# Two transformer blocks on one core: the expert routing's lists are moved behind each query part, and the expert buffers are laid out before it

## Chip, core and metric

One core of a Trainium2 chip runs the whole program. The metric is the device time of one execution in microseconds (us), the median of the runs. Names of engines: PE is TensorE (matmuls), PEld its weight loads, DVE is VectorE, ACT is ScalarE, POOL is GpSimd, SP is SyncE, which issues nearly all transfers.

## What is computed

Two transformer blocks in a row over 512 tokens of 1024 features, in float32. The first block mixes tokens by neighbourhood attention and a gated recurrence (HGRN2), and then applies a feed-forward part of 16384 experts with product keys (PEER). The change lies in this last part, in the reference:

```python
q = (t @ wq).reshape(128, 8, 2, 128)                      # queries: 8 heads, 2 halves
s = jnp.einsum('tpcd,pckd->tpck', q, sub_keys)            # scores against 128 sub-keys per half
s1, i1 = lax.top_k(s[:, :, 0], 16)
s2, i2 = lax.top_k(s[:, :, 1], 16)
cand = (s1[..., :, None] + s2[..., None, :])...           # 256 candidates per head
top, pos = lax.top_k(cand, 16)                            # 16 experts per head, 128 per token
g = jax.nn.softmax(top, axis=-1)
a = jax.nn.gelu(jnp.einsum('tpkd,td->tpk', u[idx], t), approximate=False)
return jnp.einsum('tpk,tpkd->td', (g * a), v[idx])
```

The modulation vectors of both blocks (products of a conditioning vector with `w_mod` and `w_ada`) are computed between other work. The second block (stick-breaking attention and latent attention) follows and isn't touched.

## The kernel before

The tokens are four blocks of 128 (`b` 0 to 3). Three of them (`ND` = 3, blocks 0 to 2) go through all experts densely: for each of 128 groups `e` of 128 experts, `s_part(e)` loads the group's `uT`, splits it into a high part (ACT, L190) and a low part (DVE, L191), and takes 24 matmuls of 384 columns, whose GELU is `S`. The first 88 groups' `S` are stored to DRAM (`sd`), the rest stay in the `NS` buffers of the pool `sbufS`. Block 3 is gathered: `gather` fetches the rows of `u` and `v` of its 128 experts per token with indirect transfers from POOL (`uv`, four buffers), and DVE takes the dot products and the weighted sums.

Every fp32 weight is loaded in tiles of 512 KB into a ring of four buffers named `wr` and split into `wh` and `wl`, rings of four as well. `wload` uses it for the queries' weights, `s_part` for the experts' `uT`, the last stage for `v`. A `wr` buffer comes free when its tile is split.

The order in the program is: three products (`EARLY` = 3); then eight query parts `j`, each with 48 matmuls of 512 columns (`pqT`), the scores of the four blocks (`keysT`, copied to `rsc` by ACT), and, for odd `j`, one modulation vector by `gemv_T`, whose eight weight tiles come through a ring of its own (`wg`, two buffers), two halves being summed in PSUM, copied to `row` by ACT and turned into columns by matmuls with `pick`; then 49 products up to `PRE` = 52; then the routing of blocks 3, 2, 1, 0. Routing takes the 16 best of each of a block's 16 lists (`top16`: five DVE operations and three loads of match values), then of the candidates, then the softmax (an Exp on ACT, L780), and transposes what it selected (`sel`, `gt_`) on PE into `selT`. Next is the one-hot stage (`pG`, 12 parts, with three products and one pair of gathered experts each), which builds the dense gate matrix and stores it to DRAM (`gd`); then some products ahead of the last stage; then the last stage (`po`): 128 groups of 18 matmuls of 512 columns with `v`.

The Tile scheduler makes each engine's queue at compile time from a model of its own. The program's order is the priority: an instruction that has its inputs and a buffer by that model is taken before all that stand behind it in the program. On the chip each queue runs in that order, and an instruction that waits holds up all behind it. `tc.issue_after(x)` puts what it encloses behind `x` on the engine of `x`.

A pool's memory is taken when it is opened and given back when it is closed; `reuse_waits="tile"` makes a new tile wait only for the old tiles under it. In the kernel before, the pool of the gather buffers is opened after the routing's pool `eR` is closed, so that they share memory.

Of the kernel before, what the change touches and what calls it, by code (L numbers as in the profile page):

```python
# [18 lines left out]
P = 128  # L19
# [3 lines left out]
D = 1024  # L23
KT = D // P
# [97 lines left out]
DRAM = bass.MemoryType.DRAM  # L122
BF16 = mybir.dt.bfloat16
NDENSE = 3
NS = 10
NSP = 88
PRE = 52
GEN = 3
GR = 1
LAST = 4  # L130
MOD_ORDER = (0, 5, 1, 6, 2, 7, 3, 4)
EARLY = 3
# [3 lines left out]
def program(tc, a, out, tap=None):  # L136
# [35 lines left out]
    DMA.dma_start(cs.rearrange("p a b -> p (a b)"), a["cs"])  # L172
    DMA.dma_start(vecs, a["vecs"])

    def mm(ps, lhs, rhs, first=True, last=True):
        PE.matmul(ps, lhs, rhs, start=first, stop=last)  # L176

    class Split:
        def __init__(self, hi, lo):
# [64 lines left out]
        for i in range(4):  # L244
            mm(ps[32 * i:32 * i + 32, :], cvec[:, 3 * (k0 + i):3 * (k0 + i) + 32], w[:, i, :], k0 == 0, k0 == 4)

    def gemv_T(pl, ps_pool, wname, part, v, slot, bias, tag="pm"):
        row = pl.tile([P, D], F32, name="row", bufs=1)
        for h2 in range(2):
            ps = ps_pool.tile([P, 512], F32, name=tag)  # L250
            for h in range(2):
                hf = 2 * h2 + h
                for k0 in (0, 4):
                    w = pl.tile([P, 4, GW], F32, name="wg", bufs=2)
                    DMA.dma_start(w.rearrange("p k n -> p (k n)"), a[wname][4 * part + hf][:, k0 * GW:(k0 + 4) * GW])
                    gemv_rows(ps[:, h * GW:(h + 1) * GW], w, k0)
            S.copy(row[:, h2 * 512:(h2 + 1) * 512], ps)
        ps = ps_pool.tile([P, 512], F32, name=tag)[:, :2 * KT].rearrange("p (k o) -> p k o", o=2)
        for kt in range(KT):
            mm(ps[:, kt, :], row[:, kt * P:(kt + 1) * P], pick[:, v:v + 2])  # L260
        V.tensor_add(modT[:, slot, :], ps[:, :, 0], bias)

    def bcast(ps_pool, dst, colT):
        for hf in range(2):
# [418 lines left out]
    def s_part(e, elo=None):  # L683
        u_ = wpool["w"].tile([P, KT, P], F32, name="wr")
        DMA.dma_start(u_.rearrange("p a b -> p (a b)"), a["uT"][e])
        hi = wpool["w"].tile([P, KT, P], F32R, name="wh")
        lo = wpool["w"].tile([P, KT, P], F32R, name="wl")
        split(u_, hi, lo, S.copy, elo)
        ps = pS.tile([P, 512], F32, name="pS3")
        for kt in range(KT):  # L690
            mm(ps[:, :nd], hi[:, kt, :], h2T.hi[:, kt, :nd], kt == 0, False)
            mm(ps[:, :nd], hi[:, kt, :], h2T.lo[:, kt, :nd], False, False)
            mm(ps[:, :nd], lo[:, kt, :], h2T.hi[:, kt, :nd], False, kt == KT - 1)
        r = sbuf.tile([P, nd], F32, name="S")
        S.activation(r, ps[:, :nd], AF.Gelu)  # L695
        return r

    for e in range(EARLY):
        DMA.dma_start(sd[e], s_part(e, V.tensor_tensor))
    eR = ExitStack()  # L700
    tp = pool(eR, "tp2", 1, PSUM)
    pm = pool(eR, "pm2", 4, PSUM)
# [10 lines left out]
    V.memset(zer, 0.0)  # L713

    def top16(src, w, val, pos):
        t = r2.tile([P, P], F32, name="mr", bufs=2)[:, :w]
        V.max(val[:, 0:8], src)
        V.max_index(pos[:, 0:8], val[:, 0:8], src)
        V.match_replace(t, val[:, 0:8], src, -3e38)
        V.max(val[:, 8:16], t)  # L720
        V.max_index(pos[:, 8:16], val[:, 8:16], t)

    REG = ((0, 1, 16, 0), (1, 3, 8, 16), (4, 4, 4, 40), (8, 8, 1, 56))

    def routing(b, sc):
        sv = r2.tile([P, 16, 16], F32, name="sv", bufs=2)
        si = r2.tile([P, 16, 16], U32, name="si", bufs=2)
        for j in range(16):
            top16(sc[:, j, :], P, sv[:, j, :], si[:, j, :])
        sif = r2.tile([P, 8, 2, 16], BF16, name="sif")  # L730
        V.tensor_copy(sif.rearrange("p a b c -> p (a b) c"), si)
        cand = r2.tile([P, 8, 64], F32, name="cand")
# [34 lines left out]
        V.tensor_copy(abb.rearrange("p s h k -> p s (h k)"), ab)  # L767
        sel = []
        for s_ in range(2):
            eq = r2.tile([P, 8, 16, 16], BF16, name="eq", bufs=2)  # L770
# [4 lines left out]
            t = r2.tile([P, 8, 16], F32, name=f"sel{s_}")  # L775
# [8 lines left out]
        gt_ = gate[b] if b in gate else r2.tile([P, P], F32, name="gt_")  # L784
        V.tensor_tensor(gt_.rearrange("p (h k) -> p h k", k=16), tm, ts_[:, :, None].to_broadcast([P, 8, 16]), op=OP.mult)
        if b in idx:
            V.scalar_tensor_tensor(sel[0], sel[0], 128.0, sel[1], op0=OP.mult, op1=OP.add)
            V.tensor_copy(idx[b], sel[0])
        else:
            ps = tp.tile([P, 512], F32, name="tp").rearrange("p (k c) -> p k c", k=4)  # L790
            for j, t in enumerate((sel[0], sel[1], gt_)):
                PE.transpose(ps[:, j, :], t, ident)
            S.copy(selT[b], ps[:, :3, :])

    scs = [rb.tile([P, 16, P], F32, name=f"rsc{i}") for i in range(NB)]
    for j in range(8):
        qT = r2.tile([P, 2, T], F32, name="pqT", bufs=2)
        w = wload("wq", j)
        for m in range(2):
            ps = pm.tile([P, 512], F32, name="pm")  # L800
            proj_T(ps, w, m * P, P, h2T, 0, T)
            S.copy(qT[:, m, :], ps)
        for i in range(NB):
            ps = pm.tile([P, 512], F32, name="pm")
            for m in range(2):
                mm(ps[:, m * P:(m + 1) * P], qT[:, m, i * P:(i + 1) * P], keysT[:, 2 * j + m, :])
            S.copy(scs[i][:, 2 * j:2 * j + 2, :].rearrange("p a b -> p (a b)"), ps[:, :GW])
        if j == 1:
            gemv_T(rb, tp, "w_mod", 5, 0, 5, bmT[:, 40:48], "tp")
        elif j % 2:  # L810
            part = j // 2 - 1
            gemv_T(rb, tp, "w_ada", part, 2, 6 + part, baT[:, part * 8:part * 8 + 8], "tp")
    V.scalar_tensor_tensor(modT[:, 7, :], modT[:, 7, :], 1.0, ng2T, op0=OP.add, op1=OP.mult)
    V.tensor_mul(modT[:, 7, :], modT[:, 7, :], nfT)
    for e in range(EARLY, PRE):
        DMA.dma_start(sd[e], s_part(e))
    for b in reversed(range(NB)):
        routing(b, scs[b])
    eR.close()

    ug = pool(eM, "uvg", 1)
    nfB = ug.tile([P, D], F32, name="nfB")
    DMA.dma_start(nfB, a["rows"][0:1, :].to_broadcast([P, D]))
    S.activation(nfB, nfB, AF.Square)
    gt2 = ug.tile([P, D], F32, name="gt2")
    eU = ExitStack()
    up = pool(eU, "uv", 4)
    acc = {b: ug.tile([P, D], F32, name=f"pacc{b}") for b in range(ND, NB)}
    dts = {b: ug.tile([P, P], F32, name=f"dts{b}") for b in range(ND, NB)}
    scr = ug.tile([P, D], F32, name="pscr")  # L830
    for b in acc:
        V.memset(acc[b], 0.0)
    GRP = 2

    def gather(b, j0):
        tl = []
        for j in range(j0, j0 + GRP):
            uv = up.tile([P, 2 * D], F32, name="uv")
            G.indirect_dma_start(out=uv, out_offset=None, in_=a["uv"], in_offset=bass.IndirectOffsetOnAxis(ap=idx[b][:, j:j + 1], axis=0))  # L839
            V.scalar_tensor_tensor(scr, uv[:, :D], 1.0, h2g[b], op0=OP.mult, op1=OP.mult, accum_out=dts[b][:, j:j + 1])  # L840
            tl.append(uv)
        ds_ = dts[b][:, j0:j0 + GRP]
        S.activation(ds_, ds_, AF.Gelu)
        V.tensor_mul(ds_, ds_, gate[b][:, j0:j0 + GRP])
        for j in range(j0, j0 + GRP):
            V.scalar_tensor_tensor(acc[b], tl[j - j0][:, D:], dts[b][:, j:j + 1], acc[b], op0=OP.mult, op1=OP.add)  # L846

    todo = [(b, j0) for b in range(ND, NB) for j0 in range(0, P, GRP)]
    prog = [0]

    def run_gather(upto):
        for k in range(prog[0], min(upto, len(todo))):
            gather(*todo[k])
        prog[0] = max(prog[0], upto)

    with ExitStack() as es:
        gg = pool(es, "ggen", 2)
# [2 lines left out]
        for b in range(ND):  # L860
            i1_, i2_, g_ = (selT[b][:, k, :] for k in range(3))
            for tg in range(4):
# [40 lines left out]
    with ExitStack() as es:  # L903
# [16 lines left out]
        for n, e in enumerate(order):  # L920
# [346 lines left out]
```

## Time and profile before

| | |
|---|---|
| median of 3 runs | 2346.18 us (2343.89 to 2346.5) |
| profiled execution | 2337.86 us, span 2336.1 us |
| mean granted clock of TensorE | 0.992 |
| PE busy | 97% of the span |
| DVE, ACT, POOL busy | 68%, 42%, 11% |

The profile is of one execution. Busy shares are means over stages with different limits. The matmuls are pipelined and their ends are modelled, so PE's idle time in a stretch, and the count of its matmuls there, say more than its busy share.

### The profile page before, as it was taken

Reading aid. Unit: us, or ns where it says so; the run is one execution under the profiler, and the core shown is the slowest. Engines: PE = TensorE matmul, PEld = TensorE weight load, DVE = VectorE, ACT = ScalarE, POOL = GpSimd, SP = SyncE. Lnnn points to the kernel's source line nnn. Section 1 sums busy time; section 2 is a strip of 40 time slices with the busy share of each in tenths; the row PEclk is TensorE's granted clock in tenths of the full one; section 3 lists DMA queues with packets and bytes.
Section 4 is the critical chain, followed back from the end, with each engine's and each line's share of the span. In section 5 each row is a group of like instructions: output and inputs, shape, how many; then the busy total and the mean of one; then the engine's idle time right before and its main releaser. Section 6 shows DMA issues by size and latency. Waiting matters only on the chain. (4 is left out here: it accounts for less than half of the span.)

```text
span 2336.1 us, 34601 instructions
## 1 busy us (share of the span) xinstructions
PE 2259.9 (97%) x13097; PEld 1942.3 (83%) x13097; DVE 1598.4 (68%) x3193; ACT 980.3 (42%) x1828; POOL 249.1 (11%) x159
## 2 busy tenths in 40 slices
PE   7999999998999999999999999999999999989998
PEld 4899986597779999999988888888888786666888
DVE  3674723354359977999689888888898627767344
ACT  4432333333234335877534333333333434446421
POOL 0000000000000000322222222222130000000000
PEclk9999999999999999999999999999999999999999
DMA  7111135625555574999999999999997231120221
GB/s 265 55 57 55 52 118 178 212 101 178 165 196 158 163 258 153 328 320 319 333 360 396 406 347 349 354 362 363 360 380 263 88 103 42 50 86 28 98 92 55
DMA packets 170871, 481.74 MB, mean 206 GB/s; under 512 B 14864, under 2 KB 87952, under 8 KB 153168
## 3 DMA queue, kind: packets, MB, share of 16 engines
q1 hardware_dynamic: 152272, 345.31, 42.7%
q0 software_dynamic: 18432, 134.23, 14.7%
q8 instruction: 103, 1.69, 0.3%
q14 instruction: 64, 0.52, 0.1%
HBM read 431.76 MB, written 46.66 MB: 205 GB/s over the span
## 5 line engine op out<-in xcount | busy, mean ns | idle before, releaser
L191 DVE TENSOR_TENSOR wl<-wr,wh 128x1024 fp32r<-128x1024 f32 (+1 forms) x378 | 456.7, 1211 | 362.3 <-ACT wh L190 359.8
L190 ACT CAST wh<-wr 128x1024 fp32r<-128x1024 f32 (+1 forms) x378 | 394.0, 1043 | 440.4 <-PE pm L176 196.1
L176 PE MATMUL pS<-h2h,wh 128*128 128x384 f32 x1024 | 348.2, 340 | 7.3 <-ACT S L695 7.2
L176 PE MATMUL pS<-h2h,wl 128*128 128x384 f32 x1024 | 346.1, 338 | 0.0
L176 PE MATMUL pS<-h2l,wh 128*128 128x384 f32 x1024 | 345.5, 337 | 0.0
L839 POOL DMA_INDIRECT uv<-in_uv_dram,idx x128 | 225.8, 1764 | 1006.9 <-DVE pacc L846 688.8
L176 PE MATMUL po<-wl,Wh 128*128 128x512 f32 x768 | 299.6, 390 | 1.8 <-DVE wl L191 1.8
L176 PE MATMUL po<-wh,Wl 128*128 128x512 f32 x768 | 299.5, 390 | 0.0
L176 PE MATMUL po<-wh,Wh 128*128 128x512 f32 x768 | 298.9, 389 | 0.0
L176 PEld LDWEIGHTS pS<-h2h,wh 128*128 128x128 f32 x1024 | 193.4, 189 | 11.7 <-ACT S L695 8.7
L176 PEld LDWEIGHTS pS<-h2l,wh 128*128 128x128 f32 x1024 | 193.3, 189 | 2.0 <-issue 0.8
L176 PEld LDWEIGHTS pS<-h2h,wl 128*128 128x128 f32 x1024 | 193.2, 189 | 0.0
L190 ACT CAST Wh<-W 128x384 fp32r<-128x384 f32 x128 | 65.7, 513 | 267.8 <-PE po L176 162.1
L176 PE MATMUL pm<-h2h,wh 128*128 128x512 f32 x432 | 173.5, 402 | 0.2 <-ACT cr L1106 0.2
L176 PE MATMUL pm<-h2h,wl 128*128 128x512 f32 x432 | 171.8, 398 | 0.0
L176 PE MATMUL pm<-h2l,wh 128*128 128x512 f32 x432 | 171.8, 398 | 0.0
L176 PEld LDWEIGHTS po<-wl,Wh 128*128 128x128 f32 x768 | 144.1, 188 | 31.9 <-DVE wl L191 2.6
L176 PEld LDWEIGHTS po<-wh,Wl 128*128 128x128 f32 x768 | 144.1, 188 | 30.3 <-DVE Wl L191 0.3
L176 PEld LDWEIGHTS po<-wh,Wh 128*128 128x128 f32 x768 | 144.2, 188 | 29.2
L846 DVE SCALAR_TENSOR_TENSOR pacc<-uv,dts,pacc 128x1024 f32<-128x1024 f32 x128 | 163.9, 1281 | 1.9
L840 DVE SCALAR_TENSOR_TENSOR pscr<-uv,h 128x1024 f32<-128x1024 f32 x128 | 156.1, 1219 | 1.9 <-DMA uv<-in_uv_dram,idx 0.9
L191 DVE TENSOR_TENSOR Wl<-W,Wh 128x384 fp32r<-128x384 f32 x128 | 70.8, 553 | 47.9 <-ACT Wh L190 47.8
(410 smaller groups left out, 4100.6 us busy)
## 6 DMA issues: line engine op xcount, KB each, us to landing
wr<-in_uT_dram SPq DMA_DIRECT2D x128, 512.0 KB, 6.0
wr<-in_uv_dram SPq DMA_DIRECT2D x128, 512.0 KB, 7.7
gd<-stg SPq DMA_DIRECT2D x12, 2048.0 KB, 12.6
Gt<-gd SPq DMA_DIRECT2D x32, 768.0 KB, 8.4
sd<-S SPq DMA_DIRECT2D x88, 192.0 KB, 3.9
Sr<-sd SPq DMA_DIRECT2D x88, 192.0 KB, 6.8
wr<-in_w_in_dram SPq DMA_DIRECT2D x32, 512.0 KB, 3.6
wg<-in_w_mod_dram SPq DMA_DIRECT2D x32, 512.0 KB, 4.3
```

The lines of the kernel that those rows point to most:

```text
L176: PE.matmul(ps, lhs, rhs, start=first, stop=last)
L190: (ehi or S.copy)(hi, src)
L191: (elo or V.tensor_tensor)(lo, src, hi.bitcast(F32), op=OP.subtract)
L839: G.indirect_dma_start(out=uv, out_offset=None, in_=a["uv"], in_offset=bass.IndirectOffsetOnAxis(ap=idx[b][:, j:j + 1], axis=0))
L840: V.scalar_tensor_tensor(scr, uv[:, :D], 1.0, h2g[b], op0=OP.mult, op1=OP.mult, accum_out=dts[b][:, j:j + 1])
L846: V.scalar_tensor_tensor(acc[b], tl[j - j0][:, D:], dts[b][:, j:j + 1], acc[b], op0=OP.mult, op1=OP.add)
```

## The change

The eight query parts with their scores stay in front, and the 16-best lists of all four blocks are now taken behind each part, not in the routing; the routing keeps what follows the lists and runs in the order 3, 0, 1, 2. The scores need eight small buffers (`rsc`, 1 KB per partition each) where they had four of 8 KB. The pools of the gather (`uv`, the sums and two broadcast rows) are opened before the routing's, and four pairs of experts are gathered ahead of the one-hot stage (`G0`). The transposes of blocks 0, 1 and 2 are put behind the products 34, 44 and 51 on PE. To make room, `sbufS` has 6 buffers for 10, the modulation's weight tiles go through `wr` (in the routing stage; in the attention stage they keep `wg`), `row` is half as wide and each half is turned into columns before the next half begins, the dot product is written over the gathered row, and some small tiles have one buffer for two, or two for one (`sel`, `gt_`).

```diff
-NS = 10
+NS = 6
+G0 = 4
+G1 = G0 + GR * 4 * NDENSE
+BORDER = (3, 0, 1, 2)
+NLIST = 8
+HOLD = (34, 44, 51)
...
+        last_mm[0] = PE.matmul(ps, lhs, rhs, start=first, stop=last)
...
-    def gemv_T(pl, ps_pool, wname, part, v, slot, bias, tag="pm"):
-        row = pl.tile([P, D], F32, name="row", bufs=1)
+    def gemv_T(pl, ps_pool, wname, part, v, slot, bias, tag="pm", share=False):
...
-                    w = pl.tile([P, 4, GW], F32, name="wg", bufs=2)
+                    w = wpool["w"].tile([P, 4, GW], F32, name="wr") if share else pl.tile([P, 4, GW], F32, name="wg", bufs=2)
...
-            S.copy(row[:, h2 * 512:(h2 + 1) * 512], ps)
-        ps = ps_pool.tile([P, 512], F32, name=tag)[:, :2 * KT].rearrange("p (k o) -> p k o", o=2)
-        for kt in range(KT):
-            mm(ps[:, kt, :], row[:, kt * P:(kt + 1) * P], pick[:, v:v + 2])
-        V.tensor_add(modT[:, slot, :], ps[:, :, 0], bias)
+            row = pl.tile([P, 512], F32, name="row", bufs=1)
+            S.copy(row, ps)
+            ps = ps_pool.tile([P, 512], F32, name=tag)[:, :KT].rearrange("p (k o) -> p k o", o=2)
+            for k in range(4):
+                mm(ps[:, k, :], row[:, k * P:(k + 1) * P], pick[:, v:v + 2])
+            V.tensor_add(modT[:, slot, 4 * h2:4 * h2 + 4], ps[:, :, 0], bias[:, 4 * h2:4 * h2 + 4])
...
+    ug = pool(eM, "uvg", 1)
...
+    up = pool(eU, "uv", 4)
...
-            V.scalar_tensor_tensor(scr, uv[:, :D], 1.0, h2g[b], op0=OP.mult, op1=OP.mult, accum_out=dts[b][:, j:j + 1])
+            V.scalar_tensor_tensor(uv[:, :D], uv[:, :D], 1.0, h2g[b], op0=OP.mult, op1=OP.mult, accum_out=dts[b][:, j:j + 1])
...
     eR = ExitStack()
...
-    def routing(b, sc):
-        sv = r2.tile([P, 16, 16], F32, name="sv", bufs=2)
-        si = r2.tile([P, 16, 16], U32, name="si", bufs=2)
-        for j in range(16):
-            top16(sc[:, j, :], P, sv[:, j, :], si[:, j, :])
+    def routing(b):
+        sv, si = svs[b], sis[b]
...
-            for j, t in enumerate((sel[0], sel[1], gt_)):
-                PE.transpose(ps[:, j, :], t, ident)
+            with tc.issue_after(after[HOLD[b]].ins):
+                for j, t in enumerate((sel[0], sel[1], gt_)):
+                    PE.transpose(ps[:, j, :], t, ident)
...
-        for i in range(NB):
+        lists = []
+        for i in BORDER:
...
-            S.copy(scs[i][:, 2 * j:2 * j + 2, :].rearrange("p a b -> p (a b)"), ps[:, :GW])
+            sc = r2.tile([P, 2, P], F32, name="rsc", bufs=NLIST)
+            S.copy(sc.rearrange("p a b -> p (a b)"), ps[:, :GW])
+            lists.append((i, sc))
...
-            gemv_T(rb, tp, "w_ada", part, 2, 6 + part, baT[:, part * 8:part * 8 + 8], "tp")
+            gemv_T(rb, tp, "w_ada", part, 2, 6 + part, baT[:, part * 8:part * 8 + 8], "tp", True)
+        for i, sc in lists:
+            for m in range(2):
+                top16(sc[:, m, :], P, svs[i][:, 2 * j + m, :], sis[i][:, 2 * j + m, :])
...
     for e in range(EARLY, PRE):
         DMA.dma_start(sd[e], s_part(e))
-    for b in reversed(range(NB)):
-        routing(b, scs[b])
+        after[e] = last_mm[0]
+    for b in BORDER:
+        routing(b)
+    run_gather(G0)
     eR.close()
...
-                    run_gather(GR * (b * 4 + tg + 1))
+                    run_gather(G0 + GR * (b * 4 + tg + 1))
...
-                run_gather(GR * ND * 4 - (GR * ND * 4 - len(todo)) * (n + 1) // (P - 10))
+                run_gather(G1 + (len(todo) - G1) * (n + 1) // (P - 10))
```

## Rows read from the trace of the kernel before

**Rows 1.** The page, part 1: busy us, share, instructions.

```profile
PE 2259.9 (97%) x13097; PEld 1942.3 (83%) x13097; DVE 1598.4 (68%) x3193; ACT 980.3 (42%) x1828; POOL 249.1 (11%) x159
```

**Rows 2.** Stretches: length, busy PE PEld DVE ACT POOL (instructions), clock, DMA share, GB/s.

```profile
547.50:697.50 150.00, 145.64 (x896) 109.85 (x894) 61.57 (x288) 46.00 (x80) 0.00 (x0) 1.00 0.54 177
697.50:840.00 142.50, 139.12 (x793) 138.48 (x794) 141.92 (x643) 54.39 (x73) 5.48 (x4) 0.99 0.54 163
840.00:905.00 65.00, 65.00 (x378) 64.65 (x377) 33.35 (x69) 22.43 (x32) 0.00 (x0) 1.00 0.64 230
905.00:935.00 30.00, 27.58 (x180) 26.30 (x179) 28.00 (x36) 25.18 (x56) 1.84 (x2) 1.00 0.50 166
935.00:1145.00 210.00, 209.79 (x1434) 206.48 (x1433) 195.71 (x202) 168.31 (x415) 63.39 (x21) 1.00 0.95 324
...
1260.00:1800.00 540.00, 540.00 (x2536) 465.89 (x2535) 475.61 (x656) 202.38 (x314) 129.10 (x85) 1.00 0.94 359
```

**Rows 3.** Groups of PE instructions, 560 to 700 us: the modulation's matmuls.

```profile
L176 PE MATMUL tp<-wg,cvec 128*32 128x256 f32 x248 | 21.0, 389 | 4.4 <-DMA wg<-in_w_ada_dram 2.9 <-DMA wg<-in_w_mod_dram 1.4
```

**Rows 4.** ACT in order of time at the third Exp of the routing.

```profile
784.27 1.28 ACT L780 ACT_TABLE_LOAD   x1
791.48 0.31 ACT L780 ACTIVATE tm<-tm 128x128 f32<-128x128 f32 x1 [5.92 <-DVE tm L779]
```

**Rows 5.** Stretches around idle time of PE, columns as in rows 2.

```profile
466.00:468.00 2.00, 0.25 (x3) 0.13 (x2) 0.83 (x2) 2.00 (x5) 0.00 (x0) 1.00 0.89 297
468.00:472.00 4.00, 4.00 (x22) 4.00 (x23) 4.00 (x7) 3.45 (x7) 0.00 (x0) 0.57 0.63 246
790.00:795.00 5.00, 1.70 (x10) 1.38 (x9) 5.00 (x31) 3.50 (x5) 0.00 (x0) 1.00 0.48 157
795.00:800.00 5.00, 5.00 (x22) 5.00 (x21) 5.00 (x21) 0.85 (x2) 0.00 (x0) 0.66 0.45 109
```

**Rows 6.** PE in order of time: waits at the one-hot stage's start and end.

```profile
923.85 2.53 PE L176 MATMUL pG<-Rh,Lq 128*128 128x128 f32 x16 [0.98 <-ACT Lq L879]
927.45 0.44 PE L176 MATMUL pS<-h2h,wh 128*128 128x384 f32 x1 [1.07 <-ACT S L695]
...
1169.36 0.45 PE L176 MATMUL pS<-h2h,wh 128*128 128x384 f32 x1 [2.81 <-ACT S L695]
```

**Rows 7.** Groups of DVE instructions, 550 to 950 us: count, busy us, mean ns, idle before.

```profile
L191 DVE TENSOR_TENSOR wl<-wr,wh 128x1024 fp32r<-128x1024 f32 x70 | 85.1, 1218 | 101.6 <-ACT wh L190 101.4
...
L718 DVE FIND_INDEX8 si<-sv,rsc 128x8 uint32<-128x128 f32 x64 | 18.1, 283 | 0.0
...
L717 DVE MAX8 sv<-rsc 128x8 f32<-128x128 f32 x64 | 16.1, 281 | 8.9 <-ACT rsc L807 8.9
...
L846 DVE SCALAR_TENSOR_TENSOR pacc<-uv,dts,pacc 128x1024 f32<-128x1024 f32 x4 | 5.1, 1276 | 0.0
L840 DVE SCALAR_TENSOR_TENSOR pscr<-uv,h 128x1024 f32<-128x1024 f32 x4 | 4.9, 1219 | 0.0
```

**Rows 8.** ACT in order of time around the modulation vector of part 1.

```profile
572.37 1.05 ACT L190 CAST wh<-wr 128x1024 fp32r<-128x1024 f32 x1 [1.67 <-PE pm L176]
...
578.92 0.59 ACT L257 COPY row<-tp 128x512 f32<-128x512 f32 x1 [2.98 <-PE tp L176]
```

**Rows 9.** PE in order of time, the same place.

```profile
573.16 1.06 PE L176 MATMUL tp<-wg,cvec 128*32 128x256 f32 x14
574.16 1.38 PE L176 MATMUL pm<-keysT,pqT 128*128 128x128 f32 x10
578.22 0.64 PE L176 MATMUL tp<-wg,cvec 128*32 128x256 f32 x8 [0.83 <-DMA wg<-in_w_mod_dram]
...
590.42 1.84 PE L176 MATMUL tp<-pick,row 128*128 128x2 f32 x16
```

**Rows 10.** SP's queue in order of time, last stage, groups 11 and 12.

```profile
1213.52 0.33 SPq L931 DMA_DIRECT2D wr<-in_uv_dram  x1
1217.54 0.33 SPq L685 DMA_DIRECT2D wr<-in_uT_dram  x1
```

**Rows 11.** DMA issues, 547.5 to 697.5 us: count, KB, median us to landing.

```profile
wr<-in_uT_dram SPq DMA_DIRECT2D x10, 512.0 KB, 4.7
wr<-in_wq_dram SPq DMA_DIRECT2D x9, 512.0 KB, 4.7
```

More of the change, by code (lines that the diff above doesn't have):

```diff
@@ L173, in program @@
     DMA.dma_start(vecs, a["vecs"])
+    last_mm = [None]
     def mm(ps, lhs, rhs, first=True, last=True):
-        PE.matmul(ps, lhs, rhs, start=first, stop=last)
+        last_mm[0] = PE.matmul(ps, lhs, rhs, start=first, stop=last)
     class Split:
@@ L699, in program, with gather, run_gather @@
         DMA.dma_start(sd[e], s_part(e, V.tensor_tensor))
+    ug = pool(eM, "uvg", 1)
+    nfB = ug.tile([P, D], F32, name="nfB")
+    DMA.dma_start(nfB, a["rows"][0:1, :].to_broadcast([P, D]))
+    S.activation(nfB, nfB, AF.Square)
+    gt2 = ug.tile([P, D], F32, name="gt2")
+    acc = {b: ug.tile([P, D], F32, name=f"pacc{b}") for b in range(ND, NB)}
+    eU = ExitStack()
+    up = pool(eU, "uv", 4)
+    ux = pool(eU, "uvx", 1)
+    dts = {b: ux.tile([P, P], F32, name=f"dts{b}") for b in range(ND, NB)}
+    for b in acc:
+        V.memset(acc[b], 0.0)
+    GRP = 2
+    def gather(b, j0):
+        tl = []
+        for j in range(j0, j0 + GRP):
+            uv = up.tile([P, 2 * D], F32, name="uv")
+            G.indirect_dma_start(out=uv, out_offset=None, in_=a["uv"], in_offset=bass.IndirectOffsetOnAxis(ap=idx[b][:, j:j + 1], axis=0))
+            V.scalar_tensor_tensor(uv[:, :D], uv[:, :D], 1.0, h2g[b], op0=OP.mult, op1=OP.mult, accum_out=dts[b][:, j:j + 1])
+            tl.append(uv)
+        ds_ = dts[b][:, j0:j0 + GRP]
+        S.activation(ds_, ds_, AF.Gelu)
+        V.tensor_mul(ds_, ds_, gate[b][:, j0:j0 + GRP])
+        for j in range(j0, j0 + GRP):
+            V.scalar_tensor_tensor(acc[b], tl[j - j0][:, D:], dts[b][:, j:j + 1], acc[b], op0=OP.mult, op1=OP.add)
+    todo = [(b, j0) for b in range(ND, NB) for j0 in range(0, P, GRP)]
+    prog = [0]
+    def run_gather(upto):
+        for k in range(prog[0], min(upto, len(todo))):
+            gather(*todo[k])
+        prog[0] = max(prog[0], upto)
     eR = ExitStack()
@@ L715, in top16 @@
     def top16(src, w, val, pos):
-        t = r2.tile([P, P], F32, name="mr", bufs=2)[:, :w]
+        t = r2.tile([P, P], F32, name="mr", bufs=1)[:, :w]
         V.max(val[:, 0:8], src)
@@ L723, in program @@
     REG = ((0, 1, 16, 0), (1, 3, 8, 16), (4, 4, 4, 40), (8, 8, 1, 56))
-    def routing(b, sc):
-        sv = r2.tile([P, 16, 16], F32, name="sv", bufs=2)
-        si = r2.tile([P, 16, 16], U32, name="si", bufs=2)
-        for j in range(16):
-            top16(sc[:, j, :], P, sv[:, j, :], si[:, j, :])
+    svs = [rb.tile([P, 16, 16], F32, name=f"sv{b}") for b in range(NB)]
+    sis = [rb.tile([P, 16, 16], U32, name=f"si{b}") for b in range(NB)]
+    def routing(b):
+        sv, si = svs[b], sis[b]
         sif = r2.tile([P, 8, 2, 16], BF16, name="sif")
@@ L769, in routing @@
         for s_ in range(2):
-            eq = r2.tile([P, 8, 16, 16], BF16, name="eq", bufs=2)
+            eq = r2.tile([P, 8, 16, 16], BF16, name="eq", bufs=1)
             V.tensor_tensor(eq, abb[:, s_][:, :, None, :].to_broadcast([P, 8, 16, 16]), iob[:, None].to_broadcast([P, 8, 16, 16]), op=OP.is_equal)
@@ L774, in routing @@
                 V.tensor_tensor(eq[:, :, 0:w, :], eq[:, :, 0:w, :], eq[:, :, w:2 * w, :], op=OP.add)
-            t = r2.tile([P, 8, 16], F32, name=f"sel{s_}")
+            t = r2.tile([P, 8, 16], F32, name=f"sel{s_}", bufs=2)
             V.tensor_tensor(t, eq[:, :, 0, :], eq[:, :, 1, :], op=OP.add)
@@ L783, in routing @@
         V.reciprocal(ts_, ts_)
-        gt_ = gate[b] if b in gate else r2.tile([P, P], F32, name="gt_")
+        gt_ = gate[b] if b in gate else r2.tile([P, P], F32, name="gt_", bufs=2)
         V.tensor_tensor(gt_.rearrange("p (h k) -> p h k", k=16), tm, ts_[:, :, None].to_broadcast([P, 8, 16]), op=OP.mult)
@@ L790, in routing @@
             ps = tp.tile([P, 512], F32, name="tp").rearrange("p (k c) -> p k c", k=4)
-            for j, t in enumerate((sel[0], sel[1], gt_)):
-                PE.transpose(ps[:, j, :], t, ident)
+            with tc.issue_after(after[HOLD[b]].ins):
+                for j, t in enumerate((sel[0], sel[1], gt_)):
+                    PE.transpose(ps[:, j, :], t, ident)
             S.copy(selT[b], ps[:, :3, :])
-    scs = [rb.tile([P, 16, P], F32, name=f"rsc{i}") for i in range(NB)]
     for j in range(8):
@@ L806, in program @@
                 mm(ps[:, m * P:(m + 1) * P], qT[:, m, i * P:(i + 1) * P], keysT[:, 2 * j + m, :])
-            S.copy(scs[i][:, 2 * j:2 * j + 2, :].rearrange("p a b -> p (a b)"), ps[:, :GW])
+            sc = r2.tile([P, 2, P], F32, name="rsc", bufs=NLIST)
+            S.copy(sc.rearrange("p a b -> p (a b)"), ps[:, :GW])
+            lists.append((i, sc))
         if j == 1:
-            gemv_T(rb, tp, "w_mod", 5, 0, 5, bmT[:, 40:48], "tp")
+            gemv_T(rb, tp, "w_mod", 5, 0, 5, bmT[:, 40:48], "tp", True)
@@ L810, in program @@
         elif j % 2:
             part = j // 2 - 1
-            gemv_T(rb, tp, "w_ada", part, 2, 6 + part, baT[:, part * 8:part * 8 + 8], "tp")
+            gemv_T(rb, tp, "w_ada", part, 2, 6 + part, baT[:, part * 8:part * 8 + 8], "tp", True)
+        for i, sc in lists:
+            for m in range(2):
+                top16(sc[:, m, :], P, svs[i][:, 2 * j + m, :], sis[i][:, 2 * j + m, :])
     V.scalar_tensor_tensor(modT[:, 7, :], modT[:, 7, :], 1.0, ng2T, op0=OP.add, op1=OP.mult)
     V.tensor_mul(modT[:, 7, :], modT[:, 7, :], nfT)
+    after = {}
@@ L815, in program @@
     for e in range(EARLY, PRE):
         DMA.dma_start(sd[e], s_part(e))
-    for b in reversed(range(NB)):
-        routing(b, scs[b])
+        after[e] = last_mm[0]
+    for b in BORDER:
+        routing(b)
+    run_gather(G0)
     eR.close()
[L821 to L839, printed above, removed]
-            V.scalar_tensor_tensor(scr, uv[:, :D], 1.0, h2g[b], op0=OP.mult, op1=OP.mult, accum_out=dts[b][:, j:j + 1])
[L841 to L854, printed above, removed]
     with ExitStack() as es:
```

## The prediction

> **What bounds the kernel now.** I read the page first. PE is busy for 97% of the span [rows 1], so what the change can gain is PE's idle time where it acts, and what it can lose is new idle time there. The table of stretches shows where that idle time lies [rows 2]: 4.4 us of 150 in the queries (547.5 to 697.5), 3.4 of 142.5 while DVE does the routing (697.5 to 840, DVE at 141.92 of 142.50), none up to 905, 2.4 of 30 at the start of the one-hot stage, 0.2 of 210 in the rest of it, none from 1260 to 1800. DVE has 61.57 of 150 us in the queries and is full in the routing: lists that move from the second stretch to the first go from a full DVE to one that is 41% busy.
>
> Each of the three idle places has a cause that can be read. In the queries, PE waits 4.4 us in all for weight tiles of the modulation vectors [rows 3]. At 790, PE stops because ACT's queue stands still: it has loaded the Exp table at 784.27 and waits 5.92 us for DVE's `tm` [rows 4]; no split and no GELU gets past it, and PE is busy for 1.70 of the next 5 us, with the clock at 0.66 in the 5 us after that [rows 5]. At 923 and 927, PE waits for ACT's one-hot columns and for a GELU behind them [rows 6].
>
> **What each part does.** *The lists behind each query part.* Their five DVE operations for 64 lists take between 16.1 and 18.1 us each in sum [rows 7], at most 5 x 18.1 = 91 us, or 11.3 per query part, before the short loads of match values and less what they overlap. With two low splits of 1.22 us a part needs about 13.8 us of DVE. PE takes 150 / 8 = 18.8 us per part [rows 2]; four parts hold a modulation vector of 8 x 0.64 + 1.84 = 7 us [rows 9], so a part without one takes at most (150 - 28) / 8 = 15.2 us. DVE keeps up, with little to spare on the even parts. In the routing, the 142 us that DVE works now lose at most 91 us of lists and keep about half. The third Exp should then not find DVE 6 us behind, and the stop goes: 3.3 us of idle time, and the lowered clock after it (0.34 of 5 us, 1.7 us): -5.0. The Exps and their table loads stay four. If DVE still lags as much, the stop stays: the gain is between 0 and 5.0, and I take 5.0, since half of the load is gone.
>
> *Order 3, 0, 1, 2, two buffers for `sel`, and the transposes behind products 34, 44 and 51.* Now block 0 comes last and the one-hot stage needs it first. Afterwards its `selT` is there 17 products before the stage. That takes away the idle time at its start: -2.4 at most, 0 at least, since the one-hot buffers still lie under the routing's and wait for block 2's transposes. The three products of the stage's first part (24 matmuls of 65 / 378 = 0.172 us, 4.1 us each [rows 2]) cover 12 us of preparation, so I take -2.4. The nine transposes cost PE what they do now.
>
> *Gather buffers first, eight experts ahead.* DVE and POOL do the same work earlier. From 1260 to 1800 PE has no idle time with DVE at 475.61 of 540 us [rows 2], so less gathering there gives nothing back. Eight rows of experts ahead are 8 x (1.28 + 1.22) = 20 us of DVE [rows 7], in a place where it is idle for 32 of 65 us (840 to 905 [rows 2]). Cost 0; without that cover, with DVE's queue standing at a gather that has not landed, up to 5 us, as much as the stop at 790.
>
> *Six `S` buffers.* Six products, not ten, lie ahead of the last stage: 25 us of cover for storing and re-loading the gate matrix. PE already stops there for 2.81 us [rows 6]. With less cover the stop can move or grow; with another queue order it can go. From -2.8 to +5 (again the stop at 790); I take 0.
>
> *`row` in halves in the attention stage.* Three modulation vectors get one more hand-over of the single PSUM buffer each: copy 0.59 [rows 8], four turns (half of 1.84 [rows 9]) and an addition, 1.7 us with it, beside attention work on PE. Between 0 and 5; I take +1, near the hidden end, since nothing waits for these vectors at once.
>
> *The modulation's tiles in `wr`.* This part decides. A buffer of the ring goes to the waiting transfer that stands first in the program: in the last stage the twelve loads of `v` that stand ahead of the first `uT` are all issued before it, the last at 1213.52, the `uT` at 1217.54 [rows 10]. Now the queries' loads run ahead of PE, since the modulation has its own two buffers. After the change the eight tiles of part `j` stand in the same ring ahead of the weights of part `j`+1, and unlike a weight, which leaves `wr` as soon as it is split, they leave it only when PE has used them, which PE does in gaps between scores (14 entries, under two tiles, at 573.16 [rows 9]; about three by the end of an odd part's scores). So PE then has no weights for the next part, and none can be loaded before the second half's first tile is used. From the end of the scores: the fourth tile 0.64 [rows 9] and the hand-off to ACT, to 1.0; `row` 0.59 [rows 8], to 1.6; hand-off and four turns 0.9, to 2.8; addition and hand-off, to 3.3; the fifth tile 0.64, to 3.9; the weight's transfer 4.7 [rows 11] and its issue, to 8.7; the high split 1.05 [rows 8], to 9.8; then PE can start, and stops after two matmuls for most of the low split (1.22 [rows 7]), another 0.7. In those 9.8 us PE has five tiles of 0.64 and two times 0.95 of turns, 5.1 us. Idle: 4.7 + 0.7 = 5.4 us, four times (behind part 7 it is the expert's `uT`, 4.7 us too): 21.6. Such pauses can also drop the clock: after 1.75 us without work at 466 to 468 the next 4 us ran at 0.57 [rows 5], as after the stop at 790. At 1.7 us for a drop and two drops in four, 3.4 more. What goes is the 4.4 us of waiting for `wg` [rows 3]. In sum +21.6 + 3.4 - 4.4 = +20.6. The bounds: -4.4, if PE always finds the next weights, and 4 x (5.4 + 1.7) - 4.4 = +24.
>
> The Trainium skill's page "DMA: Bandwidth & Descriptors", section "Anatomy of one DMA — SWDGE (gpsimd) path", gives a fixed 2.0 us and bytes over 436 GB/s; for 512 KB that is an estimate of 3.2 us where the trace has 4.7 [rows 11]. By it each pause would be 1.5 us shorter and the whole sum 6 us smaller, still slower than before; the page's fit is for transfers issued from GpSimd, these come from SP, and the row decides.
>
> **Sum.** -5.0 - 2.4 + 0 + 0 + 1 + 20.6 = +14.2 us. The profiled execution took 2337.86 us (span 2336.1 and 1.8 around it), 8.3 under the median of the runs; it becomes 2352, and the median 2346.18 + 14.2 = 2360.
>
> **Rivals.** *Faster: the ring doesn't bind.* If the scheduler places enough of the modulation's tiles in gaps, or the second half's tiles before the scores, the next weights are in time. Then all three idle places go: -4.4 - 5.0 - 2.4 = -11.8, 2334 us; with the stop at 1169 gone too, 2331. For it speaks that four buffers are more than two, against it that PE's queue now takes only about three tiles in the gaps. It decides where a pause costs under 11.8 / 4 = 3.0 us. Chance 0.29.
>
> *No change.* Pauses of 2 to 4 us, which take back what the routing gives: 2342 to 2350 us. Chance 0.11.
>
> *Much slower: DVE becomes the bound of the query parts too.* In the program the lists of a part stand ahead of the next weights' splits. If a low split comes behind eight lists, an even part waits as well, some 3 to 4 us for each of four (two splits and a list operation or two), and the scores' copies wait for list buffers: 2360 + 12 to 16, up to 2376; a longer stop at the last stage's start would come on top. For it speaks 13.8 against at most 15.2 us, against it that the pauses of the odd parts give DVE time. Chance 0.12.
>
> **How the numbers follow.** The forecast, 2360 us, has 0.48; its own range is 2351 to 2369. A measurement of this kernel tells about 0.2%, 4.7 us, from no change. Faster holds the first rival, 0.29; same 0.11; slower the forecast and the third rival, 0.60. The range has to reach from the first rival's 2334 to the third's 2376.
>
> **What would show it.** In the query stretch the idle time of PE grows from 4.4 to about 22 us, in four like pauses behind parts 1, 3, 5 and 7, with PE or ACT waiting for a transfer into `wr` of `wq` or `uT`; the time from the first query to the first product behind the queries grows by some 20 us. DVE's busy time there more than doubles, ACT's wait at L780 stays under 3 us at each Exp, the products run without a stop, and the one-hot stage starts without one. I am wrong if loads of the next weights are issued before a part's scores are done, if PE waits there for DVE and not for a transfer, or if the gathers ahead hold up the splits.

## The result: 1.2% slower, and the profile after

The changed kernel takes 2371.5 us (median of 6 runs, 2370.2 to 2377.0) against 2346.3 for the kernel before: a ratio of 1.0116, with a 95% interval of 1.0097 to 1.0135, or 25.2 us more. The profiled executions lie further apart, 2371.4 against 2337.86: the profiled run of before had a mean clock of 0.992, while 65 runs of it beside the experiments had 0.981 to 0.991, so it lost less to lowered clock than its median run. Differences between traces are therefore read stage by stage.

The table of stretches of the changed kernel, cut where each stage's first matmul starts (columns as in [rows 2]): queries to the seventh expert, products, one-hot stage, and two pieces of the last stage.

```profile
545.50:730.10 184.60, 164.42 (x905) 124.51 (x905) 117.11 (x623) 46.20 (x80) 0.00 (x0) 0.86 0.43 148
730.10:927.20 197.10, 192.77 (x1109) 191.47 (x1108) 143.69 (x410) 76.44 (x107) 18.36 (x12) 1.00 0.67 234
927.20:1172.50 245.30, 245.04 (x1663) 240.77 (x1661) 225.76 (x234) 193.33 (x472) 63.01 (x22) 1.00 0.87 299
1172.50:1300.00 127.50, 120.28 (x564) 104.69 (x563) 96.49 (x135) 44.68 (x72) 33.85 (x18) 0.97 0.96 365
1300.00:1800.00 500.00, 500.00 (x2366) 433.54 (x2365) 423.07 (x578) 183.50 (x283) 122.30 (x76) 1.00 0.92 347
```

The same cuts in the kernel before:

```profile
547.60:699.20 151.60, 147.24 (x905) 111.45 (x905) 62.69 (x297) 46.00 (x80) 0.00 (x0) 1.00 0.54 177
699.20:896.30 197.10, 193.72 (x1107) 193.05 (x1107) 165.56 (x693) 73.27 (x100) 5.48 (x4) 0.99 0.59 189
896.30:1144.90 248.60, 245.97 (x1661) 241.06 (x1660) 232.31 (x246) 196.94 (x476) 65.23 (x22) 1.00 0.87 297
```

The queries grow by 33.0 us, the products by nothing, the one-hot stage shrinks by 3.3. The last stage, from there to the start of its last matmul, grows from 694.7 to 700.6; PE's idle time in it, 7.2 us, lies before 1300. The start, which the change hardly touches, is 2.1 us shorter in this execution. These are the 33.5 us by which the two spans differ. The first row shows more than a length: for the same 905 matmuls PE is idle for 20.18 us instead of 4.36, and *busy* for 17.2 us more, at a mean clock of 0.86. Half of the loss is waiting, the other half is work at half speed.

How one of the pauses comes about, behind query part 1. SP's queue of the changed kernel (start, length of a run of issues, what is issued):

```profile
573.14 1.76 SPq L261 DMA_DIRECT2D wr<-in_w_mod_dram  x4
578.43 4.69 SPq L205 DMA_DIRECT2D wr<-in_wq_dram  x4
586.72 4.09 SPq L261 DMA_DIRECT2D wr<-in_w_ada_dram  x4
```

and PE in order of time, where [rows 9] showed it before:

```profile
570.61 0.62 PE L183 MATMUL tp<-wr,cvec 128*32 128x256 f32 x2
571.16 1.38 PE L183 MATMUL pm<-keysT,pqT 128*128 128x128 f32 x10
572.47 1.92 PE L183 MATMUL tp<-wr,cvec 128*32 128x256 f32 x28
575.08 1.05 PE L183 MATMUL tp<-pick,row 128*128 128x2 f32 x8 [0.69 <-ACT row L264]
577.29 2.26 PE L183 MATMUL tp<-wr,cvec 128*32 128x256 f32 x16 [1.17 <-DVE sv L759]
580.39 1.08 PE L183 MATMUL tp<-wr,cvec 128*32 128x256 f32 x8 [0.83 <-DMA wr<-in_w_mod_dram]
...
583.49 1.86 PE L183 MATMUL tp<-pick,row 128*128 128x2 f32 x8 [0.76 <-ACT row L264]
585.21 0.77 PE L183 MATMUL pm<-h2h,wh 128*128 128x512 f32 x1
...
587.07 0.63 PE L183 MATMUL pm<-h2h,wl 128*128 128x512 f32 x1
```

No weight of part 2 is asked for until 578.43, 1.1 us after PE starts on the vector's second half. The last score is 5.9 us back by then, and the first matmul of part 2 starts at 585.21. The clock has fallen in between: the four turns of a half (eight matmul records) take 1.05 us at 575.08 and 1.86 at 583.49. What PE waits for in the whole query stretch, 545.5 to 730.1 (total, times, longest):

```profile
PE tp L183 <- DMA wr<-in_w_ada_dram: 9.1, 11, 3.0
PE tp L183 <- ACT row L264: 5.9, 8, 0.8
PE pS L183 <- DVE wl L198: 1.9, 1, 1.9
PE tp L183 <- DVE sv L759: 1.2, 1, 1.2
PE tp L183 <- DMA wr<-in_w_mod_dram: 1.0, 2, 0.8
PE tp L183 <- DVE sv L762: 1.0, 1, 1.0
```

None of these waits is for a query weight: the first matmul of part 2 follows the vector's last turn without a gap, and so it is in the other three places. What costs time is that PE has nothing but the vector to work on: its second half's tiles are asked for only from 573.14, and their transfers and the copies of `row` lie open, where in the kernel before the next part's matmuls stood between them. The stretches before and in the four falls of the clock:

```profile
569.80:576.50 6.70, 5.64 (x55) 3.86 (x54) 3.87 (x26) 2.44 (x6) 0.00 (x0) 1.00 0.32 95
576.50:590.20 13.70, 11.04 (x52) 6.44 (x53) 11.37 (x45) 4.56 (x5) 0.00 (x0) 0.50 0.84 309
615.00:620.90 5.90, 3.35 (x48) 1.91 (x40) 5.30 (x37) 0.67 (x2) 0.00 (x0) 1.00 0.76 252
620.90:631.10 10.20, 8.52 (x41) 5.07 (x38) 7.44 (x28) 3.81 (x5) 0.00 (x0) 0.50 0.80 298
655.00:661.80 6.80, 4.84 (x54) 3.17 (x54) 5.36 (x37) 1.85 (x5) 0.00 (x0) 1.00 0.48 152
661.80:675.50 13.70, 9.83 (x43) 5.83 (x44) 9.65 (x37) 4.57 (x5) 0.00 (x0) 0.50 0.77 266
699.00:706.20 7.20, 4.70 (x54) 3.03 (x53) 5.90 (x40) 1.85 (x5) 0.00 (x0) 1.00 0.59 200
706.20:719.90 13.70, 9.79 (x46) 6.56 (x46) 12.76 (x78) 4.76 (x5) 0.00 (x0) 0.50 0.76 258
```

Four times PE works in pieces with small gaps and then runs for 10.2 to 13.7 us at 0.50, the 1.2 GHz level. In these four stretches it is busy for 39.2 us; at full clock half of that would do, an estimated 19.6, which is near the 17.2 by which its busy time grew.

### The profile page after: what moved, and what is told of

Read it like the earlier page. It is cut to its first block, busy times and chain, and to the rows that moved or that the text cites. A ratio compares the mean times of both kernels' runs of the same rounds, so it can differ in the third digit from the quotient of the medians.

```text
span 2369.6 us, 34596 instructions
## 1 busy us (share of the span) xinstructions
PE 2278.3 (96%) x13097; PEld 1953.7 (82%) x13097; DVE 1608.4 (68%) x3200; ACT 980.4 (41%) x1828; POOL 261.1 (11%) x159
## 5 line engine op out<-in xcount | busy, mean ns | idle before, releaser
L725 POOL DMA_INDIRECT uv<-in_uv_dram,idx x128 | 237.5, 1856 | 1031.6 <-DVE pacc L732 762.9
L726 DVE SCALAR_TENSOR_TENSOR uv<-uv,h 128x1024 f32<-128x1024 f32 x128 | 153.7, 1218 | 4.3 <-DMA uv<-in_uv_dram,idx 4.3
```

Source lines behind the costliest of these rows:

```text
L726: V.scalar_tensor_tensor(uv[:, :D], uv[:, :D], 1.0, h2g[b], op0=OP.mult, op1=OP.mult, accum_out=dts[b][:, j:j + 1])
```

## The experiments

The theory to test (T1): the vector's tiles stand in the ring ahead of the next weights, and the pauses bring lowered clock with them. The rivals: T2, the lists in the query parts hold up the low splits; T3, the row in halves makes the vectors slower. For each kernel, the table gives the stretch from the first query matmul to the seventh expert, as the rows above have it, and the times. From the third row on, a ratio is to runs of the kernel before that were taken beside that kernel's own; their medians lie between 2344.1 and 2345.4 us.

| kernel | stretch | PE busy | PE idle | median us | ratio to before (95%) |
|---|---|---|---|---|---|
| before | 151.6 | 147.24 | 4.36 | 2346.3 | |
| the change | 184.6 | 164.42 | 20.18 | 2371.5 | 1.0116 (1.0097 to 1.0135) |
| before, shared ring | 193.2 | 167.85 | 25.35 | 2383.5 | 1.0173 (1.0146 to 1.0200) |
| before, shared ring and halves | 187.8 | 163.51 | 24.29 | 2373.2 | 1.0117 (1.0096 to 1.0137) |
| the change, own tiles | 155.8 | 148.59 | 7.21 | 2345.0 | 1.0006 (0.9989 to 1.0024) |
| the change, weights ahead | 159.7 | 151.33 | 8.37 | 2345.3 | 1.0010 (0.9995 to 1.0026) |
| before, lists alone | 152.1 | 147.13 | 4.97 | 2341.2 | 0.9984 (0.9960 to 1.0008) |
| even parts, weights ahead | 149.9 | 146.12 | 3.78 | 2340.6 | 0.9978 (0.9967 to 0.9990) |

**Shared ring alone,** on the kernel before:

```
...
-                    w = pl.tile([P, 4, GW], F32, name="wg", bufs=2)
+                    w = wpool["w"].tile([P, 4, GW], F32, name="wr") if share else ...
...
```

> The kernel before, with one part of the change alone: the four late modulation vectors take their weight tiles from the ring of the query weights (the two tiles of their own are gone). Main theory (T1, the shared ring makes the next query weight's transfer start only when the vector's tiles are used up, and the pauses bring lowered clock): the time from the first query product to the first expert product grows by 25 to 35 us, and the whole run by about as much, to 2370 to 2382 us, whatever the lists do. Rival T2 (the lists in the query parts hold up VectorE's splits): there are no lists in the query parts here, so 2346 us, no change. Rival T3 (the row in halves with its copies makes the vectors slower): the row is whole here, so at least 10 us less of growth than the change shows.

It was 39 us slower, more than the whole change, and the stretch grew by 41.6 us, more than T1 had said. So the shared ring is enough by itself, and T2 can't be the cause: no lists run here.

**The vectors' own tiles given back,** on the changed kernel (`gemv_T` without `share` again, `NLIST` 7).

> The changed kernel, with the two weight tiles of their own given back to the late modulation vectors (and 7 instead of 8 score buffers, to make room). T1: the pauses behind the query parts 1, 3, 5 and 7 go, the span from the first query product to the first expert product falls by about 33 us, and the time goes to about 2338 us, ratio to before about 0.997. T2: the pauses stay, at 2365 us or more. T3: the vectors still cost 3 us each more than before, 2350 us.

Of the 33 us in the stretch, 28.8 went, and the run came back to the time of before, not under it. What stays over before is 4.2 us in the stretch and the 5.6 us of the last stage, which the ring doesn't touch.

**The ring as changed, the next weight ahead of the vector:**

```
...
+        if j in (1, 3, 5):
+            ahead[j + 1] = wload("wq", j + 1)
         if j == 1:
             gemv_T(rb, tp, "w_mod", 5, 0, 5, bmT[:, 40:48], "tp", True)
...
```

> The changed kernel with the shared ring as it is, but the query weight of parts 2, 4 and 6 is requested ahead of the modulation vector behind parts 1, 3 and 5. Nothing else is moved. T1 (the order of the requests in the ring is the cost): the pauses behind parts 1, 3 and 5 go, the one behind part 7 stays, about 2348 us. T2 and T3 (lists; halves of the row): no change from the changed kernel, about 2371 us. If instead the number of tiles in the ring is the limit, the vector's own tiles wait longer and half or less of the 23 us comes back.

This is the sharpest of the four. It has the same ring, the same number of buffers, the same lists and the same halves; only the order of requests differs, and 26 us go. The windows of this run up to the last vector, and over it:

```profile
543.50:669.80 126.30, 125.44 (x740) 94.77 (x739) 89.77 (x469) 34.31 (x63) 0.00 (x0) 1.00 0.47 159
669.80:703.20 33.40, 25.89 (x168) 20.51 (x167) 27.32 (x154) 11.47 (x17) 0.00 (x0) 0.80 0.65 218
```

With the weights ahead, PE is idle for 0.9 us up to the last query product, at a clock of 1.00; behind part 7, where nothing was put ahead, 7.5 us of idle time and the lowered clock are still there. The Trainium skill, "Perfetto Trace Analysis", section "Optimization Strategy", says that a gap which repeats on the engine that should be full can mean that no memory is left for the next tile (buffer count, tile sizes). Here the gap did come from tiles waiting for a buffer, but the number of buffers and the tile sizes stayed as they were and the gap went: it was the order in which they were asked for.

**The lists alone,** on the kernel before (`top16` behind each part's scores, order 3, 0, 1, 2, two buffers of `sel` and `gt_`).

> The kernel before, with the lists alone: each query part's lists of all four blocks behind its scores, order of blocks 3, 0, 1, 2, doubled tiles of the selected numbers; no shared ring, the row whole, gather buffers where they were, ten buffers for the scores of the experts. T1: no pause in the query parts, the stop at the Exp near 790 us (5 us with its lowered clock) goes and the one-hot start gains 2 to 3 us: 2338 to 2342 us. T2: the query parts get 20 us longer or more, about 2365 us. If the gathers laid ahead, and not the lists, are what kept the products from gaining in the changed kernel, the products from the seventh to the fifty-second expert take 4 to 5 us less here than before.

The query parts don't get longer (152.1 us), so T2 falls. But the products gain nothing either: the stretch from the seventh to the fifty-third expert is 197.0 us, though DVE works only 133.61 us in it, as against 165.56. ScalarE's queue in this run shows why; it is the place of [rows 4]:

```profile
792.42 0.48 ACT L695 ACTIVATE S<-pS 128x384 f32<-128x384 f32 x1
792.92 1.28 ACT L780 ACT_TABLE_LOAD   x1
799.72 0.31 ACT L780 ACTIVATE tm<-tm 128x128 f32<-128x128 f32 x1 [5.52 <-DVE tm L779]
```

DVE has a fifth less to do, and an Exp still waits 5.52 us: the four Exps now stand behind the GELUs of products 5, 12, 18 and 24 in ScalarE's queue, where before they stood behind 4, 13, 25 and 53, and DVE is not ready there either. The one-hot stage gains its 3.3 us here (245.3 us as after), without the held transposes and with the gather buffers in their old place.

**Six score buffers alone,** on the kernel before (`NS = 6`), and **no gathers ahead,** on the changed kernel (`G0 = 0`).

> The kernel before with one number changed: six score buffers of the experts instead of ten. In the changed kernel the stretch from the end of the one-hot stage to the last product of the last stage is 700.7 us against 694.7 before. If the six buffers are the reason (theory N), this stretch grows here to about 700 us and the run to about 2350 us; if the pace of the gathers is the reason (theory G), it stays at 694 to 695 us and the run at 2344 us. My forecast put nothing on either.

> The changed kernel with no gathers ahead of the one-hot stage (the first eight are asked for one at a time beside it, as in the kernel before). If these gathers are what stops the products at 832 and 842 us (theory G), the products from the seventh to the fifty-third expert take about 193 us instead of 197 and the last stage falls by up to 6 us: 2362 to 2367 us. If the stops come from the Exps' place in ScalarE's queue, as the kernel with the lists alone suggests (its stop at the Exp is still 5.5 us), the products stay at 196 to 197 us, and with theory N the last stage stays at 700 us: 2371 us.

From the end of the one-hot stage to the start of the last stage's last matmul, the first takes 703.2 us and the second 701.1, against 694.7 before and 700.6 after: theory N, the buffers. The first is also 0.22% slower as a whole (0.06 to 0.39%). The waits of PE in its last stage, 1152.5 to 1280 us (total, times, longest):

```profile
PE po L176 <- ACT Wh L190: 7.9, 2, 5.7
PE po L176 <- DVE Wl L191: 0.3, 1, 0.3
```

Before, PE waited there for a GELU and for DVE's split, 4.6 us in all; with six products in hand it waits for the cast of the weighted scores. In the changed kernel the like stop, 3.0 us at 1220, follows a wait of DVE of 5.29 us for the scores' transfer back (`Sr`). Without gathers ahead the products still take 197.5 us, so taking the gathers out gives nothing. That doesn't mean that they held up nothing. In the changed kernel PE stops three times in the products, for 1.38, 1.44 and 1.51 us, at 793, 832 and 842 us, and before each of them ScalarE's queue stood at a gather's GELU (`dts`), which waits for VectorE as the Exp does; before the last two:

```profile
828.77 0.20 ACT L729 ACTIVATE dts<-dts 128x2 f32<-128x2 f32 x1 [3.65 <-DVE uv L726]
...
842.06 0.20 ACT L729 ACTIVATE dts<-dts 128x2 f32<-128x2 f32 x1 [7.25 <-DVE uv L726]
```

The Exp behind the first of the two waits only 0.15 us, and no Exp stands near the second; at 793 a gather's GELU (4.60 us) and an Exp (2.96) come one after the other. Without the gathers the last Exp stands three products earlier in the queue, waits 7.01 us, and PE stops once, for 3.45 us. The one kind of stop takes the other's place. The time of this run, 2376.3 us (1.0126, 1.0104 to 1.0147), is no better than that of the change.

**All vectors at even parts, all weights ahead,** on the changed kernel:

```
...
-        if j == 1:
+        if j % 2 == 0:
+            ahead[j + 1] = wload("wq", j + 1)
+        if j == 0:
             gemv_T(rb, tp, "w_mod", 5, 0, 5, bmT[:, 40:48], "tp", True)
-        elif j % 2:
+        elif j % 2 == 0:
...
```

> The changed kernel with all four late vectors moved to the query parts 0, 2, 4 and 6, and the query weight of the next part requested ahead of each vector, so that no vector stands in front of a weight in the ring. T1: the last pause of the run with three weights ahead (17 us between the last query product and the fourth expert, 2 us before the change) goes as well: 10 to 13 us less than that run, 2332 to 2336 us, ratio to before 0.995 to 0.997. If the ring is too small for a vector beside the weights, part of a pause comes back behind each vector: 2340 us or more.

The last pause went from the stretch, as T1 says, and with it 4.7 us of the median (7.5 by the ratios to the kernel before) and not 10 to 13. The other case, that part of a pause comes back, isn't seen: PE idles 3.78 us, less than before the change. The products took 201.3 us in this execution, 4.4 more than in the run with three weights ahead: ScalarE's Exps waited 14.2 us for DVE in it, and 6.7 in the other, and PE was idle for 6.6 us against 4.2.

**The same with ten score buffers and no gathers ahead** (`NS = 10`, `G0 = 0`).

> As the kernel with the vectors at the even parts and the weights ahead, and ten score buffers again and no gathers ahead of the one-hot stage. If these two numbers are what cost the last stage 4 to 6 us, it falls to 695 us: 2328 to 2332 us, ratio to before about 0.994. If not, the time is that of the kernel with even parts, 2332 to 2336 us.

2332.6 us, ratio 0.9947 (0.9930 to 0.9963), just outside what the first case gave. The last stage falls to 690.4 us, less than before the change; the two numbers were not told apart here.

**The Exps held,** on that kernel and on the kernel before. Each Exp gets an order edge behind a later GELU on ScalarE's queue; nothing is computed otherwise:

```
...
+EXPAT = (16, 23, 30, 9)
...
-        S.activation(tm, tm, AF.Exp)
+        with tc.issue_after(behind[EXPAT[b]].ins):
+            S.activation(tm, tm, AF.Exp)
...
```

> The fastest kernel so far (even parts, weights ahead, ten score buffers, no gathers ahead) with one edit: ScalarE's four Exps of the gates are queued behind the GELUs of the products 16, 23, 30 and 9, where VectorE is through with their inputs, instead of behind those of products 13, 20, 26 and 6, where ScalarE stood 4 to 8 us at each with the next products' GELUs and casts behind them. If the Exps' place in ScalarE's queue is what stops the products (theory E), the stretch from the seventh to the fifty-third expert falls from 200.4 us to 192 to 195 us and the run to 2324 to 2328 us. If VectorE's amount of work is the reason (what my forecast said), the products stop for the low halves of their weights instead, and the time stays at 2331 to 2334 us.

It is 2322.1 us, ratio 0.9908 (0.9890 to 0.9926), the fastest kernel of this study. The windows of the queries and of the products:

```profile
545.70:694.20 148.50, 146.32 (x906) 112.30 (x906) 106.49 (x541) 43.86 (x78) 0.00 (x0) 1.00 0.54 183
694.20:885.80 191.60, 191.60 (x1109) 191.57 (x1108) 137.05 (x466) 78.39 (x105) 3.99 (x4) 1.00 0.59 198
```

PE has no idle time left in the products, with the same DVE work as in the run without the edge, whose window is

```profile
693.10:893.50 200.40, 195.42 (x1109) 194.12 (x1108) 136.86 (x466) 77.44 (x105) 3.99 (x4) 0.98 0.55 189
```

8.8 us of difference from the place of four instructions, the lowered clock behind the stops included. The last of the experiments does the same to the kernel before; there the four Exps came to stand behind the products 5, 15, 28 and 53.

> The kernel before with its second and third Exp queued behind the GELUs of products 15 and 28 instead of 13 and 25, and nothing else moved; the lists stay where they were. Theory E: the stop of 3.3 us near 790 us and the lowered clock behind it go, the stretch from the seventh to the fifty-third expert falls from 197.1 us to about 192 to 194 us, 2340 to 2342 us. If VectorE's load with the lists is the reason, the stop moves and the stretch stays at 196 to 198 us.

This gave no measurable gain: 2346.3 us, 1.0002 (0.9987 to 1.0017), with 196.2 us for the products where theory E had 192 to 194. In the trace the stop at the third Exp is gone (product 20 to product 34 takes 58.8 us instead of 63.4), but 4.1 us are lost again between products 34 and 51. ScalarE's queue there:

```profile
855.76 1.06 ACT L194 CAST wh<-wr 128x1024 fp32r<-128x1024 f32 x1 [7.21 <-DMA wr<-in_uT_dram]
...
861.38 1.05 ACT L194 CAST wh<-wr 128x1024 fp32r<-128x1024 f32 x1 [4.18 <-DMA wr<-in_uT_dram]
```

The weight for the cast at 855.76 was issued at 847.77, at the end of four gathers' issue from GpSimd (842.16 to 848.6), whose first and last landed 8.7 and 14.1 us after theirs. The issues of the weight in the stretches 838 to 839, 847.7 to 848.1 and 852.9 to 853.3, with the microseconds to landing:

```profile
wr<-in_uT_dram SPq DMA_DIRECT2D x1, 512.0 KB, 3.8
...
wr<-in_uT_dram SPq DMA_DIRECT2D x1, 512.0 KB, 7.9
...
wr<-in_uT_dram SPq DMA_DIRECT2D x1, 512.0 KB, 8.3
```

Beside the gathers a weight took twice its time. The Trainium skill, "DMA: Bandwidth & Descriptors", section "Queues, rings and completion order", has each DMA engine take turns between the queues that hold work for it; the trace agrees as far as it goes, the weight being late and not stopped. That it is the gathers that delay it was read from traces and not tried by itself. Nor is the delay all of it: in the kernel before, two weights beside the same four gathers took 8.2 and 9.1 us (issued at 838.44 and 843.60), and PE didn't stop at all from 834 to 864. Why it stops here stays open.

**Shared ring and halves,** on the kernel before (the first experiment with the changed `row`).

> The kernel before with the shared ring and the row in halves, without the lists. With the shared ring alone the run was 2383.5 us, 12 us over the changed kernel, which has both. If halves of the row shorten what is exposed of each vector (theory H), this run is at the changed kernel's 2370 to 2375 us. If the halves cost (my forecast: 1 us, at most 5) or do nothing, it is at 2383 to 2388 us and the 12 us lie in the changed kernel's other parts.

Theory H: with halves the median is 10 us under that of the ring alone, 5.4 us of it in the stretch, and the two together come to the change's time without any list. T3 had the sign wrong.

## Why the prediction was right, and where its steps were off

The direction, the place and the main of the mechanism were right, and the time came out 11.5 us over the forecast. Stage by stage the traces differ by 33.5 us, 19.3 more than the forecast's 14.2; the profile of the kernel before lies 8 us under its median. Step by step:

- **The pauses.** Forecast 17.2 us more idle time (21.6 less 4.4), measured 15.8. The order in the ring was as described, in four places, with the next weights issued only after the second half's first tile. The chain behind it was not. PE took about a quarter of a tile among the scores and not three tiles, so the second half's tiles were asked for late, and the next weights 5.9 us after the scores and not 3.9. The forecast had PE wait for the next weight's transfer and counted no transfer of the vector's own tiles; of the 20.1 us of PE's waits, 10.1 are for those tiles, 5.9 for the copies of `row`, and none for a query weight (ScalarE's casts wait 4.8 us for those). That the idle time came out near the forecast is in part luck. The three experiments on the ring and the order of requests show the cause.
- **The lowered clock: the term that was mis-sized.** Forecast 3.4 us, "At 1.7 us for a drop and two drops in four". Measured: four drops in four, 10.2 to 13.7 us long, and 17.2 us more of busy time, 13.8 over the term. I took the length of a drop from two single stops [rows 5] and carried it to a place where PE works in pieces for ten microseconds. This is most of what the forecast missed in the traces.
- **The Exp stop, -5.0: a step that failed.** I read the Exp's wait for DVE's `tm` as DVE having too much to do, and expected that "the stop goes" once half of its load was gone. With the lists alone moved, the Exp still waited 5.52 us. ScalarE's queue is in an order fixed beforehand, and the Exp stands in it before DVE can have its input; when the lists left, the Exps moved up with the rest of the routing. Held behind a later GELU, in the kernel without gathers ahead, the stops vanish though DVE's work is the same. After the change the Exps wait 3.0 and 3.6 us at the most costly two, where I had said under 3, and PE stops three times for 1.4 to 1.5 us, two of them at the gathers' GELU rather than at an Exp.
- **The one-hot start, -2.4.** Measured -3.3, for another reason than the held transposes: these ran at 927 us, behind product 51, and not 17 products ahead. The kernel with the lists alone has the same 245.3 us without the hold, so the hold isn't needed for it; whether the moved lists, the order of the blocks or the second buffers of `sel` do it was not told apart.
- **Six score buffers, 0.** Measured +5.9 in the last stage, and 8.5 for the six buffers alone on the kernel before, both over the bound of 5.
- **Row in halves, +1.** From the first projection's matmul to the first query, +0.7 us (501.8 to 502.5); behind the query parts, where the vectors stand exposed, halves save 5.4 us of the stretch. **Gathers ahead, 0:** taking them out changed no time for the better, but the forecast's own sign of being wrong, that they hold up the splits, is there: the high splits stand behind their GELU in ScalarE's queue, for 7.25 us at 842.
- **The rivals.** The ring did bind; DVE did not become the bound of the query parts. Its busy time there grew to 117.11 us, 1.9 times and not "more than doubles".

## What to carry to other kernels

A shared ring is a queue in order of requests: before tiles that are held until used are put into it, request whatever the main work needs next ahead of them. A wait on another engine at the head of an in-order queue needn't mean that the other engine is overloaded; ask first whether the waiting instruction is queued too early, and move it behind work that is ready. Price a pause on TensorE with the lowered clock behind it, which here cost as much again.

## What the runs showed of the hardware

In the four pauses PE was busy for 5.64 of 6.7, 3.35 of 5.9, 4.84 of 6.8 and 4.70 of 7.2 us before the clock fell, with single waits of 0.5 to 1.3 us there, and then had 10.2 to 13.7 us at half clock, with waits of up to 3.0 us in them; behind the single stop at 790 in [rows 5] stand 5 us at a mean of 0.66, an estimated 3.4 at half clock. Such falls also came where nothing was changed: the run with the lists alone had one of 20.5 us ahead of the queries, where its code is that of the kernel before.

```profile
380.90:397.20 16.30, 14.47 (x136) 8.07 (x135) 5.36 (x13) 7.22 (x14) 0.00 (x0) 1.00 0.69 221
397.20:417.70 20.50, 19.59 (x95) 13.63 (x94) 5.76 (x18) 6.54 (x13) 0.00 (x0) 0.50 0.54 197
```

From 380.9 us to the first query it took 11.0 us longer than the profile of before took from 380.8 (177.8 and 166.8 us). Whether such falls are all of the spread of the runs (2337 to 2358 us for the kernel before) stays open.
